# Two attention stages of a two-layer diffusion step: when a low part, a PSUM bank and a set of weights are put in the queues

## The chip, the cores and the metric

The kernel is one program on one core of a Trainium2 chip. The metric is the device time of one execution in microseconds (us), as the median of several runs. The core has five instruction streams that matter here: PE (TensorE, matrix products and transposes; PEld is its weight loads), DVE (VectorE), ACT (ScalarE), POOL (GpSimd) and SP (SyncE, which here only issues DMAs). Each takes its instructions strictly in the order of the program; they wait for each other by semaphores.

## The reference, cut to what matters

One step of a trunk of two layers over 512 latent tokens and 128 context tokens of width 1024. Layer 0 mixes tokens by 2-D neighbourhood attention (NA), layer 1 by grouped-query attention (GQA, 16 query heads over 4 key heads); a gated ConvFFN follows each.

```python
for l in range(DEPTH):                                   # DEPTH = 2
    hp = rmsnorm(xp, norm_mix_pre[l]) * (1.0 + sc_ap) + sh_ap      # context
    hs = rmsnorm(xs, norm_mix_pre[l]) * (1.0 + sc_as) + sh_as      # latents
    if l % 2 == 0:
        qp, kp, vp = na_qkv(hp, na_w_qkv[i]); op = blocked_attention(qp, kp, vp)
        qs, ks_, vs = na_qkv(hs, na_w_qkv[i])
        os_ = neighbourhood_attention(qs, ks_, vs, cache_k, cache_v, na_rpb[i])
        w_o = na_w_o[i]
    else:
        qp, kp, vp = gqa_qkv(hp, ...); op = blocked_attention(qp, kp, vp)
        qs, ks_, vs = gqa_qkv(hs, ...); qs, ks_ = axial_rope(qs), axial_rope(ks_)
        os_ = blocked_attention(qs, concat(ks_, cache_k), concat(vs, cache_v))
        w_o = gqa_w_o[i]
    xp = xp + g_ap * rmsnorm(op @ w_o, norm_mix_post[l])
    xs = xs + g_as * rmsnorm(os_ @ w_o, norm_mix_post[l])
    ...                                                  # gated ConvFFN, again with a residual
```

## The kernel before, in words

All products that carry weights or latent rows run in three passes over split numbers: a value x is held as a high part `hi` (a rounded copy, made by ACT) and a low part `lo = x - hi` (a subtraction, on DVE or POOL), and `passes` adds hi·hi, hi·lo and lo·hi. So every weight (`wsplit`: load `wr`, high part `wh`, low part `wl`) and every attention output costs one ACT copy and one subtraction before PE can use it.

PE's order is the order in which the program is written: `pe()` chains each matmul and transpose to the one before. The other engines' instructions are put in order by a scheduler from their readiness and their place in the program. Two calls bend that order, without adding a wait for data: `behind(a, b)` puts instruction a later than b on their engine, and `tc.keep_in_program_order(a)` puts it later than whatever the program wrote last for that engine. An engine runs its queue strictly in order, so what stands first and isn't ready holds back all behind it.

PSUM has eight banks of 128 x 512 f32. `Banks` hands them out first in, first out: `get` takes the bank that was returned longest ago, and `put` returns one at the place of the program where it is called. The next owner of a bank waits until the last reader of the old owner is done.

**GQA, layer 1.** After the projections four banks serve the scores (two tiles `d0` and `d1` of two banks each) and four go round among all else. The attention is cut into 32 units u: head `2*(u//4) + u%2`, half `u//2 % 2` of the latent rows. A unit has two score tiles (`scores(0)`, `scores(1)`: products `s`, DVE reduction `nmg` L1796, ACT exponential `gp` L1799, DVE reciprocal `rcg` L1801, POOL scaling `gp` L1802) and three transposes (`turns(0..2)`: 4, 4 and 2 PE turns into a bank `tp`, then a copy `pk` out of it: turn 0 by ACT L1813, turn 1 by DVE L1815, turn 2 by ACT or DVE). `GORDER` writes the order by hand:

```python
GORDER = ("s0 p v s1 t0".split(), "s0 l1 l2 t0 s1 t1 t2".split())   # even u, odd u
```

where s0, s1 are the scores of unit u + 2, t0, t1, t2 the turns of unit u, l1, l2 the last two turns of unit u - 1, p a leftover step of the query transposes or of the context attention, and v is `values`: the products of units u - 2 and u - 1 (two heads, one half) with the values, into a bank `po`. `po` is taken with the first half (`hf == 0`) and closed with the second (`hf == 1`): ACT writes the high part `ph` (L1832), DVE the low part `pl` (L1833), and the bank goes back. The list `held` carries instructions that a later `scores(i)` puts behind its reduction. The context columns of the same output come from `opr` and are split on POOL (L1840, L1841).

**NA, layer 0.** The heads' attention steps are interleaved with the projections by `ORDER`: each `f` runs one part of the queue `work` (`stream()`), whose last item is the key projection of head pair 7, in eight parts (first half of the rows in parts 0 to 3, second half in 4 to 7; `k_put` then splits the keys, `kp` is the context's key copy). At parts of this last item named in `OW` the first half of the output weights (`m0.weights(0, u)`) is split, pinned in program order. `o_split(p)` (L1097) splits the attention output of pair p into `oh` and `ol`: pairs 0 and 1 after head 11, the next after head 12, when the memory of the projections' input is free.

**First ConvFFN's end.** For the last tile of rows (t = 4) `after(i)` splits the four GQA key and value weights between the last products, while DVE and POOL finish tile 3 (`residual`, `ro` the reciprocal root, `shifted` L421).

Of the kernel before, what the change touches and what calls it, by code (L numbers as in the profile page):

```python
# [14 lines left out]
ALU = mybir.AluOpType  # L15
# [7 lines left out]
NS = 512  # L23
# [16 lines left out]
NPT = 6  # L40
NPK = 6
NAR = 2
OW = {0: 0, 2: 1, 7: 2}
OEARLY = 2
TH = 322
PLAIN = 2
# [58 lines left out]
def hybrid_step(ctx: ExitStack, tc: tile.TileContext, A, O):  # L105
# [57 lines left out]
    def x_in(t):  # L163
        return A["x_sample"][0, t * P : (t + 1) * P, :] if t < 4 else A["x_prompt"][0]

    queue, lowered = [], []


    def wsplit(src, a, b, low=None, own=None, pin=False, after=None, high=None, low_after=None):
        q = own or wp  # L170
        raw = wp.tile([P, a, b], F32, tag="wr", name="wr")
        i = nc.sync.dma_start(raw, src)
        if queue:
            behind(i, queue.pop())
        hi = q.tile([P, a, b], F32R, tag="wh", name="wh")
        i = nc.scalar.copy(hi, raw)  # L176
        lo = q.tile([P, a, b], F32R, tag="wl", name="wl")
        j = (low or nc.vector).tensor_sub(lo, raw, f32(hi))  # L178
        if high:
            behind(i, high[0])  # L180
        if after:
            behind(i, after[0])
            behind(j, after[1])
        lowered[:] = [j]
        if low_after and not low:
            behind(j, low_after)
        if pin:
            tc.keep_in_program_order(i)
            tc.keep_in_program_order(j)
        return hi, lo  # L190
# [150 lines left out]
    class Finish:  # L341
# [75 lines left out]

        def shifted(self, t):
            xm, r = self.xm[t]
            self.moved = [  # L420
                nc.vector.scalar_tensor_tensor(  # L421
                    xm[:, c], xm[:, c], r, self.sh[:, c], op0=ALU.mult, op1=ALU.add
                )
                for c in HALF
            ]
            return self.moved[0]

        def last(self, copied, added, low):

# [51 lines left out]
    vpool = l_na.enter_context(pool("nav", 3))  # L481
    tpool = l_na.enter_context(pool("nat"))
    mask = tpool.tile([P, 2, 32, 8], F32, name="mask")
    kput, plast, qput, splits = [], [], [], []
    wqkv = A["na_w_qkv"][0]

    def na_v_tile():
# [362 lines left out]
    with l_na:  # L850
# [50 lines left out]
        def na_qk_items(p):  # L901
# [20 lines left out]
            def k_put(c0, c1, src):  # L922
                for b in range(2):
                    own, oth = own_oth(b)
                    i = nc.scalar.copy(d["kh"][b][own, c0:c1], src[own])
                    j = (nc.scalar.copy if p else nc.vector.tensor_copy)(d["kh"][b][oth, c0:c1], src[own])
                    n = nc.vector.tensor_sub(d["kl"][b][own, c0:c1], src[own], f32(d["kh"][b][own, c0:c1]))
                while splits and c0 == 0:
                    for x, y in zip(splits.pop(), (j, n)):
                        behind(x, y)  # L930
                if not p:
                    kput[:] = [i]

            def part(which, half, k0):
# [12 lines left out]
                if which == 0:  # L947
                    if half == 0:
                        d["qs"] = [ap.tile([P, QW], F32R, tag=f"qs{b}", name=f"qs{b}") for b in range(2)]
                    pieces = [(slice(64 + cs.start, 64 + cs.stop), slice(0, nq))]  # L950
                    if half == 1:
                        pieces.append((slice(0, 64), slice(NS - 64 - cs.start, NS - cs.start)))
                    for qc, pc in pieces:
                        for b in range(2):
                            own, oth = own_oth(b)
                            q = d["qs"][b]
                            j = nc.scalar.activation(q[own, qc], pp[own, pc], AF.Copy, scale=-0.125)
                            i = nc.vector.scalar_tensor_tensor(
                                q[oth, qc], pp[own, pc], -0.125, f32(q[own, qc]),
                                op0=ALU.mult, op1=ALU.subtract,  # L960
                            )
                    qput[:] = j, i
                else:
                    if half == 0:
                        d["kh"] = [ap.tile([P, T + P], F32R, tag=f"kh{b}", name=f"kh{b}") for b in range(2)]
                        d["kl"] = kls[p % 2]
                        tk = bk.get("tk")
                        turn(tk[:, 0:P], d["kc"], ident)
                        k_put(CTX * P, CTX * P + P, tk[:, 0:P])
                        bk.put(tk)  # L970
                    if half == 1:
                        d["kp"] = ap.tile([P, P], F32, tag="kc", name="kp", bufs=2)
                        nc.scalar.copy(d["kp"], pp[:, NS - cs.start : T - cs.start])
                    k0 = cs.start + P * (cs.start >= CTX * P)
                    k_put(k0, k0 + nq, pp[:, 0:nq])
                    if half == 1:
                        qk_of[p] = (d["qs"], d["kh"], d["kl"])
# [116 lines left out]

        def o_split(p):
            hi, lo = osp0[p]
            i = nc.scalar.copy(hi, of0[p]), nc.vector.tensor_sub(lo, of0[p], f32(hi))  # L1097
            if p == 0:
                for j in range(2):
                    behind(i[j], qput[j])  # L1100
            elif p < OEARLY:
                splits.append(i)


        items, marks = [], {}
# [13 lines left out]
        def stream():  # L1119
            items[0][0]()  # L1120
            tail = None
            for n, (load, parts) in enumerate(items):
                for i, part in enumerate(parts):
                    part()
                    if n + 1 == len(items) and i in OW:
                        m0.weights(0, OW[i], None if i == 7 else nc.gpsimd)
                    if i == 1 and n + 1 < len(items):
                        items[n + 1][0]()
                    if i == 4 and tail:
                        tail()  # L1130
                        tail = None
                    yield
# [107 lines left out]
    def ffn(l, hT, hT_close, xold, xnew, nxt, todo, late, late_close, side, back, first, fin0, after=None):  # L1240
# [290 lines left out]
        for grp, (c0, c1) in (((0, 1, 2), HB[0]), ((3, 4), HB[1])):  # L1531
# [24 lines left out]
            for t in grp:  # L1556
# [7 lines left out]
                for i in range(tail):  # L1564
# [4 lines left out]
                        lds.append(load_dn(len(lds), *HB[1]))  # L1569
                    if t == 4 and after:  # L1570
                        after(i)
                        if not i:
                            behind(fin.moved[0], lowered[0])
                late.append(fin.end(t, acc[t][0], acc[t][1], fin.stat(acc[t][0])))
        fin.close()
        s.close()
# [186 lines left out]

        return [one, two, three]

    sps, sps_p, ta, un, held = ExitStack(), [], {}, {}, ([], [])

    class Unit:

# [34 lines left out]
        def turns(self, j):  # L1804
# [7 lines left out]
            if j == 0 or j == 2 and self.b == 0:  # L1812
                nc.scalar.copy(x, tp[:, 0:n])  # L1813
            else:
                nc.vector.tensor_copy(x, tp[:, 0:n])  # L1815
            bk.put(tp)
            for a, c in enumerate(cs):
                self.t[c] = x[:, 256 * a : 256 * a + 256]
# [1 line left out]
    def values(two):  # L1820
# [8 lines left out]
        if u.hf == 1:  # L1829
            p = u.p  # L1830
            hi, lo = osp1[p]
            nc.scalar.copy(hi[:, 0:NS], ta["po"])  # L1832
            held[0].append(nc.vector.tensor_sub(lo[:, 0:NS], ta["po"], f32(hi[:, 0:NS])))  # L1833
            bk.put(ta["po"])
            c, src = slice(NS, T), opr[:, p, :]
            if p == KC - 1:
                nc.scalar.copy(hi[:, c], src)
                nc.vector.tensor_sub(lo[:, c], src, f32(hi[:, c]))
            else:
                i = nc.gpsimd.tensor_scalar(hi[:, c], src, 1.0, None, op0=ALU.mult)  # L1840
                nc.gpsimd.tensor_sub(lo[:, c], src, f32(hi[:, c]))  # L1841
                tc.add_manual_dep(i.ins, last_rms[0].ins.name, no_sync, reason="order")

    ck = ap.tile([P, 256], F32, tag="ck", name="ck", bufs=1)
    nc.scalar.dma_start(ck, A["cache_gqa_k"][0, 0].rearrange("t h d -> t (h d)"))
# [74 lines left out]
    with ExitStack() as s:  # L1920
# [27 lines left out]
        for u in range(NU + 2):  # L1948
            if u + 2 < NU:
                un[u + 2] = Unit(u + 2)  # L1950
            for step in GORDER[u % 2]:
# [9 lines left out]
                elif step == "v" and u >= 2:  # L1961
                    values((un[u - 2], un[u - 1]))
            un.pop(u - 3, None)
            if u == WU:
                for k in range(4):
                    m1.weights(0, k, None)
# [105 lines left out]
```

## Time and profile before

| | |
|---|---|
| median of 3 runs | 1544.62 us (1543.17 to 1544.98) |
| the profiled execution | 1544.49 us, of which the recorded span is 1542.7 us |
| busy: PE, PEld | 1510.3 us (98%), 1342.4 us (87%) |
| busy: DVE, ACT, POOL | 1013.9 us (66%), 854.0 us (55%), 701.1 us (45%) |
| DMA | 243.99 MB, mean 158 GB/s |
| granted TensorE clock | 0.999 of full speed |

Where the stages lie in the span, in us: first layer's projections and attention to about 320, its output product and norms to 400, first ConvFFN to 811, GQA projections to 910, GQA attention 914 to 1037, its output product and norms to 1100, second ConvFFN to the end.

How to read the rows that follow: a row of a timeline is the start in us, the duration in us (of all merged instructions), the engine, the line of the kernel, the operation, output <- input, shapes and a count; in brackets the idle time of the engine just before it and what released it. A row of a list of waits is who waited, on whom, and then the total in us, the number of waits and the longest. A row of a table of windows is the stretch, its length, the busy time of PE, PEld, DVE, ACT and POOL with counts, the granted clock, the DMA engines' mean busy share and GB/s. When an instruction waits for several things, the releaser is the event that came last by the profile, which need not be the true one.

### The profile page before, as it was taken

The page shows a single profiled execution, that of the slowest core. Times are in us where ns is not written, and L with a number is a line of the kernel's source. Part 1 is how long each engine was busy: PE and PEld are TensorE (multiplying, and loading weights), DVE is VectorE, ACT ScalarE, POOL GpSimd, SP SyncE. Part 2 cuts the span into 40 slices and gives each one's busy share as a digit, 9 for nine tenths or more (in the row PEclk, how much of TensorE's full clock was granted, in tenths as well). Part 3 has the DMA queues.
Part 4 walks back from the last instruction along what each step waited for, and adds up shares of the span by engine and source line. Part 5 has one row for each costly group of instructions (what it writes and reads, how often), then busy time and mean ns, then how long its engine had stood idle before and what let it go on. Part 6 is the DMA issues. An engine that isn't in the chain of part 4 may idle for free.

```text
span 1542.7 us, 26131 instructions
## 1 busy us (share of the span) xinstructions
PE 1510.3 (98%) x9710; PEld 1342.4 (87%) x9710; DVE 1013.9 (66%) x1653; ACT 854.0 (55%) x1628; POOL 701.1 (45%) x602
## 2 busy tenths in 40 slices
PE   7999999999999999999999999999999999999998
PEld 5999989779999999988887877778999999998886
DVE  5544343659776676764747777672988887885454
ACT  5665564655655555644544447762666665564343
POOL 1655554332355445533544454432335666553433
PEclk9999999999999999999999999999999999999999
DMA  9755444263675664487574420005533334459664
GB/s 350 190 153 127 125 136 105 61 212 103 195 226 188 206 204 141 138 290 263 187 223 137 123 83 28 1 20 195 169 114 108 117 110 156 128 162 302 196 219 134
DMA packets 196667, 243.99 MB, mean 158 GB/s; under 512 B 11484, under 2 KB 153020, under 8 KB 196540
## 3 DMA queue, kind: packets, MB, share of 16 engines
q1 hardware_dynamic: 186924, 235.85, 47.6%
q10 hardware_dynamic: 9616, 6.48, 2.5%
q8 instruction: 76, 1.25, 0.3%
q14 instruction: 51, 0.42, 0.1%
HBM read 214.38 MB, written 26.34 MB: 156 GB/s over the span
## 4 chain that ended last, share of the span: by engine, by line
PE 64%; DVE 7%; issue 2%; POOL 2%; ACT 1%; DMA 1%; ACTq 0%; DVEq 0%; POOLq 0%
PE acc L117 19%; PE ux L117 17%; PE uz L117 9%; PE uy L117 5%; PE gp L117 3%; PE y L117 2%; PE s L117 2%; PE po L117 2%; PE tp L120 2%; PE ada L117 1%; DVE B L250 1%; DVE nmg L1796 1%; DMA gn<-in_gqa_k_norm 1%; DMA wr<-in_ffn_w_up 1%; DVE wl L178 0%
## 5 line engine op out<-in xcount | busy, mean ns | idle before, releaser
L178 POOL TENSOR_TENSOR wl<-wr,wh 128x1024 fp32r<-128x1024 f32 x70 | 171.2, 2450 | 238.5 <-ACT wh L176 238.3
L117 PE MATMUL ux<-B,wh 128*128 128x322 f32 x832 | 200.5, 312 | 0.7 <-ACT u L1349 0.4
L1294 POOL TENSOR_TENSOR wl<-wr,wh 128x1024 fp32r<-128x1024 f32 x76 | 181.5, 2410 | 42.1 <-ACT wh L1293 38.3
L1373 DVE SCALAR_TENSOR_TENSOR t<-C,cw,t 128x644 f32<-128x644 f32 x176 | 156.3, 888 | 51.2 <-ACT t L1370 50.7
L117 PE MATMUL acc<-wh,alo 128*128 128x512 f32 x440 | 172.0, 391 | 0.0
L117 PE MATMUL acc<-wh,ahi 128*128 128x512 f32 x440 | 171.9, 391 | 0.0
L117 PE MATMUL acc<-wl,ahi 128*128 128x512 f32 x440 | 171.8, 390 | 0.0
L176 ACT CAST wh<-wr 128x1024 fp32r<-128x1024 f32 x138 | 143.5, 1047 | 37.8 <-DMA wr<-in_ffn_w_down 26.0
L117 PE MATMUL uz<-B,wh 128*128 128x322 f32 x640 | 155.9, 312 | 0.0
L117 PEld LDWEIGHTS ux<-B,wh 128*128 128x128 f32 x832 | 143.5, 189 | 4.2 <-ACT u L1349 1.4
L1262 DVE TENSOR_TENSOR alo<-ain,ahi 128x384 fp32r<-128x384 f32 (+1 forms) x88 | 70.5, 819 | 94.0 <-ACT ahi L1260 93.7
L117 PE MATMUL ux<-B,wl 128*128 128x322 f32 x416 | 129.3, 311 | 0.2 <-DVE wl L799 0.2
L117 PE MATMUL qk<-hT,wh 128*128 128x384 f32 (+1 forms) x512 | 122.4, 315 | 0.0
L117 PEld LDWEIGHTS uz<-B,wh 128*128 128x128 f32 x640 | 110.9, 189 | 2.9 <-issue 0.8
L1293 ACT CAST wh<-wr 128x1024 fp32r<-128x1024 f32 x84 | 85.0, 1049 | 47.1 <-DVE wr L1318 46.7
L1294 POOL TENSOR_TENSOR vl<-wr,vh 128x1024 fp32r<-128x1024 f32 x38 | 98.5, 2593 | 20.0 <-ACT vh L1293 19.7
L178 DVE TENSOR_TENSOR wl<-wr,wh 128x1024 fp32r<-128x1024 f32 x68 | 91.3, 1352 | 19.3 <-ACT wh L176 18.7
L1370 ACT ACTIVATE t<-C,cw 128x644 f32<-128x644 f32 x88 | 78.6, 893 | 44.0 <-DVE C L1401 31.6
L1260 ACT CAST ahi<-ain 128x384 fp32r<-128x384 f32 (+1 forms) x88 | 39.7, 460 | 108.9 <-PE acc L117 96.6
L117 PE MATMUL uz<-B,wl 128*128 128x322 f32 x320 | 99.5, 311 | 0.4 <-POOL wl L1294 0.3
L117 PEld LDWEIGHTS acc<-wh,alo 128*128 128x128 f32 x440 | 82.6, 188 | 17.8
L117 PEld LDWEIGHTS acc<-wh,ahi 128*128 128x128 f32 x440 | 82.6, 188 | 17.8
(264 smaller groups left out, 3893.6 us busy)
## 6 DMA issues: line engine op xcount, KB each, us to landing
wr<-in_ffn_w_up SPq DMA_DIRECT2D x88, 512.0 KB
wr<-in_ffn_w_down SPq DMA_DIRECT2D x88, 512.0 KB
wr<-in_ada_w SPq DMA_DIRECT2D x72, 512.0 KB
act<-act SPq DMA_DIRECT2D x44, 321.0 KB
wr<-in_na_w_qkv SPq DMA_DIRECT2D x24, 512.0 KB
mod<-modrow SPq DMA_DIRECT2D x20, 512.0 KB
ain<-act SPq DMA_DIRECT2D x44, 192.0 KB
wf<-in_ada_w SPq DMA_DIRECT2D x16, 512.0 KB
```

Source lines behind the costliest of these rows:

```text
L117: pe(nc.tensor.matmul(*a, **k))
L120: pe(nc.tensor.transpose(*a, **k))
L176: i = nc.scalar.copy(hi, raw)
L178: j = (low or nc.vector).tensor_sub(lo, raw, f32(hi))
L250: return nc.vector.tensor_sub(lo, src, f32(hi))
L1260: pin(nc.scalar.copy(hi[:, 0 : c1 - c0], ain[:, 0 : c1 - c0]))
L1262: i = nc.vector.tensor_sub(lo[:, 0 : c1 - c0], ain[:, 0 : c1 - c0], f32(hi[:, 0 : c1 - c0]))
L1293: nc.scalar.copy(hl[0], src)
L1294: return low.tensor_sub(hl[1], src, f32(hl[0]))
L1370: nc.scalar.activation(t, taps(0), AF.Identity, bias=cw[:, 3, n : n + 1], scale=cw[:, 1, n : n + 1])
L1373: nc.vector.scalar_tensor_tensor(t, taps(d), cw[:, w, n : n + 1], t, op0=ALU.mult, op1=ALU.add))
L1796: self.red[i] = nc.vector.tensor_reduce(nm, sv, axis=AX.XY, op=ALU.min)
```

## The change

In GQA the low part `pl` of a closed pair is put behind the DVE copy of the next turn 1 (`held[2]`, popped in `turns` with j == 1) in place of the next reduction of `scores(0)`, and the bank of `po` is returned at the end of the odd unit that follows (`ta["old"]`). The context columns' splits on POOL are kept in program order, where they had been put behind the last reciprocal root of the projections. In NA the splits of the outputs of pairs 0 and 1 are no longer put behind the last query evictions (`qput`) and the key evictions of pair 7 (`splits`), and the third block of output weights is split after part 4 of the last item and not after part 7. At the end of the first ConvFFN `shifted` of tile 3 is no longer put behind the low part of the first key weights (`lowered`).

```diff
--- before.py
+++ after.py
@@ -40,7 +40,7 @@
 NPT = 6
 NPK = 6
 NAR = 2
-OW = {0: 0, 2: 1, 7: 2}
+OW = {0: 0, 2: 1, 4: 2}
 OEARLY = 2
 TH = 322
 PLAIN = 2
@@ -163,7 +163,7 @@
     def x_in(t):
         return A["x_sample"][0, t * P : (t + 1) * P, :] if t < 4 else A["x_prompt"][0]

-    queue, lowered = [], []
+    queue = []


     def wsplit(src, a, b, low=None, own=None, pin=False, after=None, high=None, low_after=None):
@@ -181,7 +181,6 @@
         if after:
             behind(i, after[0])
             behind(j, after[1])
-        lowered[:] = [j]
         if low_after and not low:
             behind(j, low_after)
         if pin:
@@ -417,13 +416,12 @@

         def shifted(self, t):
             xm, r = self.xm[t]
-            self.moved = [
+            return [
                 nc.vector.scalar_tensor_tensor(
                     xm[:, c], xm[:, c], r, self.sh[:, c], op0=ALU.mult, op1=ALU.add
                 )
                 for c in HALF
-            ]
-            return self.moved[0]
+            ][0]

         def last(self, copied, added, low):

@@ -481,7 +479,7 @@
     vpool = l_na.enter_context(pool("nav", 3))
     tpool = l_na.enter_context(pool("nat"))
     mask = tpool.tile([P, 2, 32, 8], F32, name="mask")
-    kput, plast, qput, splits = [], [], [], []
+    kput, plast = [], []
     wqkv = A["na_w_qkv"][0]

     def na_v_tile():
@@ -923,11 +921,8 @@
                 for b in range(2):
                     own, oth = own_oth(b)
                     i = nc.scalar.copy(d["kh"][b][own, c0:c1], src[own])
-                    j = (nc.scalar.copy if p else nc.vector.tensor_copy)(d["kh"][b][oth, c0:c1], src[own])
-                    n = nc.vector.tensor_sub(d["kl"][b][own, c0:c1], src[own], f32(d["kh"][b][own, c0:c1]))
-                while splits and c0 == 0:
-                    for x, y in zip(splits.pop(), (j, n)):
-                        behind(x, y)
+                    (nc.scalar.copy if p else nc.vector.tensor_copy)(d["kh"][b][oth, c0:c1], src[own])
+                    nc.vector.tensor_sub(d["kl"][b][own, c0:c1], src[own], f32(d["kh"][b][own, c0:c1]))
                 if not p:
                     kput[:] = [i]

@@ -954,12 +949,11 @@
                         for b in range(2):
                             own, oth = own_oth(b)
                             q = d["qs"][b]
-                            j = nc.scalar.activation(q[own, qc], pp[own, pc], AF.Copy, scale=-0.125)
-                            i = nc.vector.scalar_tensor_tensor(
+                            nc.scalar.activation(q[own, qc], pp[own, pc], AF.Copy, scale=-0.125)
+                            nc.vector.scalar_tensor_tensor(
                                 q[oth, qc], pp[own, pc], -0.125, f32(q[own, qc]),
                                 op0=ALU.mult, op1=ALU.subtract,
                             )
-                    qput[:] = j, i
                 else:
                     if half == 0:
                         d["kh"] = [ap.tile([P, T + P], F32R, tag=f"kh{b}", name=f"kh{b}") for b in range(2)]
@@ -1094,12 +1088,8 @@

         def o_split(p):
             hi, lo = osp0[p]
-            i = nc.scalar.copy(hi, of0[p]), nc.vector.tensor_sub(lo, of0[p], f32(hi))
-            if p == 0:
-                for j in range(2):
-                    behind(i[j], qput[j])
-            elif p < OEARLY:
-                splits.append(i)
+            nc.scalar.copy(hi, of0[p])
+            nc.vector.tensor_sub(lo, of0[p], f32(hi))


         items, marks = [], {}
@@ -1123,7 +1113,7 @@
                 for i, part in enumerate(parts):
                     part()
                     if n + 1 == len(items) and i in OW:
-                        m0.weights(0, OW[i], None if i == 7 else nc.gpsimd)
+                        m0.weights(0, OW[i], None if i == 4 else nc.gpsimd)
                     if i == 1 and n + 1 < len(items):
                         items[n + 1][0]()
                     if i == 4 and tail:
@@ -1569,8 +1559,6 @@
                         lds.append(load_dn(len(lds), *HB[1]))
                     if t == 4 and after:
                         after(i)
-                        if not i:
-                            behind(fin.moved[0], lowered[0])
                 late.append(fin.end(t, acc[t][0], acc[t][1], fin.stat(acc[t][0])))
         fin.close()
         s.close()
@@ -1763,7 +1751,7 @@

         return [one, two, three]

-    sps, sps_p, ta, un, held = ExitStack(), [], {}, {}, ([], [])
+    sps, sps_p, ta, un, held = ExitStack(), [], {}, {}, ([], [], [])

     class Unit:

@@ -1812,7 +1800,9 @@
             if j == 0 or j == 2 and self.b == 0:
                 nc.scalar.copy(x, tp[:, 0:n])
             else:
-                nc.vector.tensor_copy(x, tp[:, 0:n])
+                i = nc.vector.tensor_copy(x, tp[:, 0:n])
+                while j == 1 and held[2]:
+                    behind(held[2].pop(), i)
             bk.put(tp)
             for a, c in enumerate(cs):
                 self.t[c] = x[:, 256 * a : 256 * a + 256]
@@ -1830,16 +1820,15 @@
             p = u.p
             hi, lo = osp1[p]
             nc.scalar.copy(hi[:, 0:NS], ta["po"])
-            held[0].append(nc.vector.tensor_sub(lo[:, 0:NS], ta["po"], f32(hi[:, 0:NS])))
-            bk.put(ta["po"])
+            held[2].append(nc.vector.tensor_sub(lo[:, 0:NS], ta["po"], f32(hi[:, 0:NS])))
+            ta["old"] = ta.pop("po")
             c, src = slice(NS, T), opr[:, p, :]
             if p == KC - 1:
                 nc.scalar.copy(hi[:, c], src)
                 nc.vector.tensor_sub(lo[:, c], src, f32(hi[:, c]))
             else:
-                i = nc.gpsimd.tensor_scalar(hi[:, c], src, 1.0, None, op0=ALU.mult)
-                nc.gpsimd.tensor_sub(lo[:, c], src, f32(hi[:, c]))
-                tc.add_manual_dep(i.ins, last_rms[0].ins.name, no_sync, reason="order")
+                tc.keep_in_program_order(nc.gpsimd.tensor_scalar(hi[:, c], src, 1.0, None, op0=ALU.mult))
+                tc.keep_in_program_order(nc.gpsimd.tensor_sub(lo[:, c], src, f32(hi[:, c])))

     ck = ap.tile([P, 256], F32, tag="ck", name="ck", bufs=1)
     nc.scalar.dma_start(ck, A["cache_gqa_k"][0, 0].rearrange("t h d -> t (h d)"))
@@ -1961,6 +1950,8 @@
                 elif step == "v" and u >= 2:
                     values((un[u - 2], un[u - 1]))
             un.pop(u - 3, None)
+            if u % 2 and "old" in ta:
+                bk.put(ta.pop("old"))
             if u == WU:
                 for k in range(4):
                     m1.weights(0, k, None)
```

## The prediction

> **What bounds the kernel now.** I read the page's first part, then the list of TensorE's waits cut to the attention of the second layer (905 to 1035 us), then the timelines of the engines around single waits.
>
> ```profile
> PE 1510.3 (98%) x9710; PEld 1342.4 (87%) x9710; DVE 1013.9 (66%) x1653; ACT 854.0 (55%) x1628; POOL 701.1 (45%) x602
> 930.00:1000.00 70.00, 66.07 (x521) 54.08 (x518) 50.71 (x109) 49.79 (x122) 32.10 (x43) 1.00 0.05 16
> PE tp L120 <- DVE rcg L1801: 6.8, 7, 1.1
> PE tp L120 <- POOL gp L1802: 1.4, 2, 0.9
> PE s L117 <- ACT gp L1799: 0.7, 1, 0.7
> ```
>
> PE is busy 98% of the span, so only its gaps can be won. In 930 to 1000 us it is idle 3.9 of 70 us at a granted clock of 1.00, while DVE (50.7) and ACT (49.8) have room, and DMA is at 5%: work there runs by the chain between engines, not by loads. The three rows of waits list all of PE's larger gaps in this attention: 6.8 us in seven waits of one kind, 1.4 us in two of another, 0.7 us in one.
>
> One of the seven, in order of time, PE first, then DVE, ACT and POOL:
>
> ```profile
> 932.52 0.60 PE L120 MATMUL tp<-ident,gp 128*128 128x128 f32 x4
> 932.88 0.54 PE L117 MATMUL s<-gkh,gq 128*128 128x320 f32 x2
> 933.55 0.82 PE L120 MATMUL tp<-ident,gp 128*128 128x128 f32 x6
> 935.32 0.63 PE L120 MATMUL tp<-ident,gp 128*128 128x128 f32 x4 [0.95 <-DVE rcg L1801]
> 936.37 0.82 PE L120 MATMUL tp<-ident,gp 128*128 128x128 f32 x6
> 942.16 1.25 PE L120 MATMUL tp<-ident,gp 128*128 128x128 f32 x10
> 933.75 0.82 DVE L1796 TENSOR_REDUCE nmg<-s 128x1 f32<-128x640 f32 x1 [0.20 <-PE s L117]
> 934.49 0.68 DVE L1833 TENSOR_TENSOR pl<-po,ph 128x512 fp32r<-128x512 f32 x1
> 935.09 0.15 DVE L1801 RECIPROCAL rcg<-sug 128x1 f32<-128x1 f32 x1
> 935.16 0.67 DVE L1815 COPY pk<-tp 128x512 f32<-128x512 f32 x1
> 936.57 0.82 DVE L1796 TENSOR_REDUCE nmg<-s 128x1 f32<-128x640 f32 x1 [0.67 <-PE s L117]
> 933.16 0.59 ACT L1813 COPY pk<-tp 128x512 f32<-128x512 f32 x1 [0.61 <-PE tp L120]
> 935.34 1.57 POOL L1802 TENSOR_SCALAR gp<-gp,rcg 128x640 f32<-128x640 f32 x2 [2.36 <-DVE rcg L1801]
> ```
>
> Read it against the code. The x4 at 932.52 is step t0 of an even unit, the x6 at 933.55 are l1 (four turns) and l2 (two), the x4 at 935.32 is t0 of the odd unit, the x6 at 936.37 are t1 and t2. The view names rcg, but a turn reads gp, which POOL makes from rcg, and the next gp starts at 935.34, after the turn: rcg can't be its input. The bank can. Four banks go round first in, first out. Where values() closes a pair (hf = 1) it gives po's bank back at once, as the fourth in the queue: t0, l1 and l2 take the other three, and t0 of the odd unit gets po's own bank, which DVE reads until pl ends at 935.17. PE starts 0.15 us later. rcg ends at 935.24 and only happens to be the last DVE event ahead. In the odd unit of the other half of a pair (942.16, ten turns without a gap) po is held, three banks go round, and t0 gets the bank of the even t0, long copied.
>
> **The change, part by part, against this execution (1544.49 us, of which 1542.7 are the span; the median of the runs is 1544.62, 0.13 more).**
>
> *Bank one unit later, and pl behind the copy of l1.* The odd t0 then gets the bank of the even t0, which ACT has copied at 933.75; PE reaches it at 935.32 - 0.95 = 934.37. The wait goes: 7 waits, 6.8 us. What is late next: t1 takes the bank of l1. PE is there 936.37 - 935.32 = 1.05 us after t0, at 935.42. With pl out of its way, DVE copies l1 from 934.49 to 935.16, and with the 0.15 us seen above the bank is free at 935.31: 0.11 us to spare, 0.05 short if rcg goes first. I take 0.05 for each, 0.3 us in all. pl now runs behind that copy, in the 0.67 us for which DVE sat idle before 936.57; the reduction behind it starts some 0.3 us late, and who waits for it (exp, rcg, gp) is needed in the next odd unit, some 6 us later (942.16): nothing. The next po now takes another bank than its old one: in the units with an extra step p (a quarter of them at most, about five) that of t1, whose copy moves to about 936.6 to 937.25, with PE there at about 937.2: 0 to 0.25 each, I take 0.1, 0.5 in all. The last of the seven lies just ahead of the first output products, which wait for their weights already:
>
> ```profile
> 1037.62 0.50 PE L117 MATMUL y<-wl,ph 128*128 128x512 f32 x1 [0.18 <-DVE wl L178]
> ```
>
> PE would come 0.95 us earlier to a chain of splits that moves by less; I take 0.4 us off. Sum of this part: -6.8 + 0.3 + 0.5 + 0.4 = -5.6, between -6.8 and -4.0 (0.2 at every t1, 0.25 at five po, 0.9 at the end).
>
> *The context part of the output (opr) on POOL.* Today only the last rms is ahead of these splits, so those of four pairs run as soon as that is done:
>
> ```profile
> 914.44 1.04 POOL L1840 TENSOR_SCALAR ph<-opr 128x128 fp32r<-128x128 f32 x2
> 915.44 0.87 POOL L1841 TENSOR_TENSOR pl<-opr,ph 128x128 fp32r<-128x128 f32 x2
> 916.28 1.23 POOL L1840 TENSOR_SCALAR ph<-opr 128x128 fp32r<-128x128 f32 x2
> 917.48 0.86 POOL L1841 TENSOR_TENSOR pl<-opr,ph 128x128 fp32r<-128x128 f32 x2
> 918.33 3.13 POOL L1802 TENSOR_SCALAR gp<-gp,rcg 128x640 f32<-128x640 f32 x4
> 919.18 0.33 PE L120 MATMUL tp<-ident,gp 128*128 128x128 f32 x1 [0.91 <-POOL gp L1802]
> 919.96 0.55 PE L120 MATMUL tp<-ident,gp 128*128 128x128 f32 x3 [0.45 <-POOL gp L1802]
> ```
>
> Four gp stand in a queue behind 3.9 us of splits, and PE waits 0.91 + 0.45 us for the first two. In program order each pair's split stands in its own even unit, behind the gp of s0. POOL starts at 914.4 with gp, done at 916.0, before PE asks at 918.3: -1.4 us, between -1.4 and 0 (if something else is as late). In the units 1.0 us of splits fits the 2.36 us for which POOL sat idle before 935.34: nothing; without that cover seven times 1.0.
>
> *NA: splits of pairs 0 and 1 free, third weights three parts earlier.* ACT, DVE and PE at the end of the first layer's projections:
>
> ```profile
> 267.42 1.92 ACTq L862 DMA_DIRECT2D tr<-in_k_rpb  x3
> 269.38 0.49 ACT L957 ACTIVATE qs<-qk 64x384 fp32r<-64x384 f32 x1 [2.16 <-POOL p L1053]
> 273.19 0.73 ACT L1097 CAST oh<-of 128x640 fp32r<-128x640 f32 x1
> 277.98 0.72 ACT L1097 CAST oh<-of 128x640 fp32r<-128x640 f32 x1
> 278.73 0.27 ACT L973 COPY kp<-qk 128x128 f32<-128x128 f32 x1
> 282.39 1.04 ACT L176 CAST wh<-wr 128x1024 fp32r<-128x1024 f32 x1
> 283.33 1.35 ACT L1097 CAST oh<-of 128x640 fp32r<-128x640 f32 x2
> 279.05 0.33 PE L120 MATMUL tk<-ident,kp 128*128 128x128 f32 x1 [0.78 <-ACT kp L973]
> 285.93 0.50 PE L117 MATMUL y<-wh,ol 128*128 128x512 f32 x1 [1.09 <-DVE ol L1097]
> ```
>
> The weights' hi (1.04 on ACT at 282.39) and lo (on DVE behind it) stand ahead of the splits of pairs 2 and 3. Moved up, they stand behind the first half's key copies, about 278.0, and those splits come about 1 us earlier: the wait of 1.09 goes. But they now stand ahead of kp, for which PE waits 0.78 already: + 1.04, less the 0.72 of the hi at 277.98, which leaves its place: + 0.3. The raw weights are loaded long before, and no load on SP lies between the two places. The two free hi copies (0.73 + 0.72) can start once the rows of the last modulation, over whose memory they lie, are stored, near the evictions of the last queries (269.38): hidden if they fit beside the loads that ACT issues from 267.42, else these evictions and the bank they hold come up to 1.45 later. I take 0.3. Sum: -1.09 + 0.3 + 0.3 = -0.5, between -1.9 (kp gains too) and + 1.4.
>
> *First FFN's end: shifted no longer behind the first key weights.*
>
> ```profile
> 810.37 1.22 DVE L178 TENSOR_TENSOR wl<-wr,wh 128x1024 fp32r<-128x1024 f32 x1
> 812.31 1.41 DVE L421 SCALAR_TENSOR_TENSOR xm<-xm,ro,mod 128x512 f32<-128x512 f32 x2 [0.72 <-POOL ro L381]
> 813.64 3.49 DVE L178 TENSOR_TENSOR wl<-wr,wh 128x1024 fp32r<-128x1024 f32 x3
> 817.18 0.73 PE L117 MATMUL gp<-wl,hT 128*128 128x512 f32 x2 [0.40 <-DVE wl L178]
> ```
>
> shifted waits for ro until 812.3, after this split is done, so the same order stands to reason: 0. If shifted is put first, all four splits end 1.2 us later, and PE's 0.40 becomes 1.6: 0 to + 1.2.
>
> Sum: -5.6 - 1.4 - 0.5 + 0 = -7.5, and 1544.49 - 7.5 = 1537.0 us. No load of the attention limits it (DMA 5%), and the weights and rows behind it are asked for by work that moves along, so the gain lasts to the end.
>
> **Rivals.** *The name in the view is right:* the odd t0 waits for something in DVE's chain that stays, and moving pl and the bank wins nothing. For it: seven rows name rcg. Against: gp starts after the turn, and the ten turns at 942.16 need no wait. Only POOL's and NA's parts are left: 1544.5 - 1.9 = 1542.6.
>
> *Three banks are too few (slower):* po's bank is now out in nearly every unit, and in each of the 15 odd units behind the first t1 must wait for the copy of l1. It decides from (6.8 + 1.4 + 0.5) / 15 = 0.58 us a unit on; at the 0.95 that t0 pays today it costs 15 x 0.95 = 14.2 against these 8.7: 1550. Against: the ten turns at 942.16 run on three banks today with no gap. The Trainium skill's page "PSUM — Partial Sum Buffer" (Summary: rules for kernel authors) says to evacuate PSUM promptly because it is tight; this change does the opposite, and by that rule the 1550 would be the outcome. The ungapped row speaks against it here.
>
> *NA's older order costs:* the free hi copies go in front of the last query evictions and the weights in front of kp, 1.45 + 1.04 with no gain at 285.93: + 2.5 in place of - 0.5, 1540.0. For it: ACT runs without a gap there.
>
> **Chances.** Forecast 0.72 (its own range 1534 to 1540), the name is right 0.10, three banks 0.04, NA costs 0.14. The predicted time is that of the forecast. The range 1534 to 1541.8 leaves out the first two rivals and a little of the forecast's lower tail, 0.2. 0.2% is 3.1 us, about what a measurement tells from no change: faster (below 1541.5) 0.82, same 0.12, slower 0.06.
>
> **What would show it.** Of the seven waits of tp about none is left in 930 to 1035, and pl follows a pk copy; a remainder would stand at the x6 behind the odd t0. No split of opr at 914 to 918, and no wait of tp for gp at 919. In NA no wait for ol near 285.9, and kp behind a weights' hi. The prediction is wrong if t0 keeps its gap with pl moved, if gaps move to t1 or po in every unit, or if the new places on ACT open gaps in NA of more than 2 us.

## The result: 1535.55 us, and the profile after

| | before | after |
|---|---|---|
| median of 6 runs each, on one chip | 1544.36 us (1543.17 to 1545.60) | 1535.55 us (1534.39 to 1536.63) |
| the profiled execution: time, span | 1544.49, 1542.7 us | 1535.05, 1533.3 us |

The ratio is 0.9943, with a 95% interval of 0.9930 to 0.9956: 8.8 us less. The forecast was 7.5 less, 1537.0.

The first part of the page, then the stretch of 70 us of the attention that answers to 930 to 1000 of before, then the whole list of PE's waits from 900 to 1031 us, all of the changed kernel:

```profile
PE 1511.8 (99%) x9710; PEld 1344.4 (88%) x9710; DVE 1016.9 (66%) x1653; ACT 853.2 (56%) x1628; POOL 703.1 (46%) x602
927.00:997.00 70.00, 69.51 (x540) 56.74 (x538) 53.86 (x115) 52.11 (x129) 34.85 (x47) 1.00 0.05 16
PE s L117 <- ACT gp L1787: 0.7, 1, 0.7
PE y L117 <- DVE wl L178: 0.2, 1, 0.2
```

PE's idle time in the 70 us fell from 3.9 to 0.5 us at the same clock. Of the three rows of before, the seven waits named rcg and the two for gp are gone; the single wait of s (0.7) stands as it was. (In the rows of the changed kernel the line numbers are lower, by 10 to 12 in the attention: L1787 is L1799 of before, L1803 is L1815, L1823 is L1833; and by 1 to 6 in the stages ahead of it.)

The same pair of units as in the prediction, from the timelines of the changed kernel; PE, then its weight loads, DVE and POOL:

```profile
929.20 1.25 PE L120 MATMUL tp<-ident,gp 128*128 128x128 f32 x10
931.04 0.87 PE L120 MATMUL tp<-ident,gp 128*128 128x128 f32 x6
...
931.03 0.64 PEld L120 LDWEIGHTS tp<-ident,gp 128*128 128x128 f32 x6 [0.22 <-DVE pk L1803]
933.02 1.92 PEld L117 LDWEIGHTS po<-pk,gvt 128*64 128x64 f32 x20 [0.32 <-DVE pk L1803]
...
930.29 0.69 DVE L1803 COPY pk<-tp 128x512 f32<-128x512 f32 x1
930.90 0.68 DVE L1823 TENSOR_TENSOR pl<-po,ph 128x512 fp32r<-128x512 f32 x1
931.49 0.15 DVE L1789 RECIPROCAL rcg<-sug 128x1 f32<-128x1 f32 x1
931.56 0.81 DVE L1784 TENSOR_REDUCE nmg<-s 128x1 f32<-128x640 f32 x1
932.29 1.01 DVE L1803 COPY pk<-tp 128x512 f32<-128x512 f32 x2
...
928.61 0.54 POOL L1830 TENSOR_SCALAR ph<-opr 128x128 fp32r<-128x128 f32 x1
929.23 0.46 POOL L1831 TENSOR_TENSOR pl<-opr,ph 128x128 fp32r<-128x128 f32 x1
```

The six turns l1, l2 and the four of t0, two groups with 0.95 us between them before, are one row of ten without a gap. pl follows the copy of l1, and rcg follows pl: rcg now ends at 931.64, 1.2 us *after* the tenth turn, so it never was what t0 waited for. What is late next are the weight loads of t1 (x6) and of po, which wait 0.2 and 0.3 us for copies.

**A ledger.** PE runs the same 9710 instructions in the same order in both kernels, so the starts of each can be subtracted, and every gap that goes or comes is a step in the difference:

| place (time before) | step, us |
|---|---|
| start-up, to 33 us | +1.1 |
| NA, 273.8 to 291.8 | -1.9 |
| 355 | -0.2 |
| two turns of the GQA projections, 836.8 and 843.7 | -1.5 |
| first units of the attention, 919.2 and 920.0 | -1.8 |
| the rest of the attention: seven gaps -7.9, given back between them +2.7 | -5.2 |
| all other | 0.0 |
| end | -9.5 |

The start-up differs from one execution to the next: at 262 us the traces of e1 to e6 below, which leave it alone, are 0.3 to 1.6 us later than that of before. A part of it is the clock: from 20.0 to 23.5 us the granted clock was 1.00 in before's trace and 0.51 in that of the changed kernel.

PE's waits from 262 to 300 us (NA), before and then after:

```profile
PE y L117 <- DVE ol L1097: 1.1, 1, 1.1
PE tk L120 <- ACT kp L973: 0.8, 1, 0.8
PE tp L120 <- POOL pp L771: 0.7, 1, 0.7
PE sp L117 <- DVE kl L927: 0.2, 1, 0.2
```
```profile
PE tp L120 <- DVE qs L953: 1.0, 1, 1.0
PE tp L120 <- POOL p L1047: 0.5, 1, 0.5
PE tk L120 <- ACT kp L967: 0.2, 1, 0.2
```

Four waits, 2.8 us, became three of 1.7. The new one, for qs, is that of the queries behind the two free copies, as the timeline of ACT after shows:

```profile
269.83 0.73 ACT L1091 CAST oh<-of 128x640 fp32r<-128x640 f32 x1 [1.58 <-POOL p L1047]
270.47 0.48 ACT L952 ACTIVATE qs<-qk 64x384 fp32r<-64x384 f32 x1
270.86 0.71 ACT L1091 CAST oh<-of 128x640 fp32r<-128x640 f32 x1
272.04 0.49 ACT L952 ACTIVATE qs<-qk 64x384 fp32r<-64x384 f32 x1 [0.47 <-DVE qs L953]
...
279.24 1.05 ACT L176 CAST wh<-wr 128x1024 fp32r<-128x1024 f32 x1
280.31 0.27 ACT L967 COPY kp<-qk 128x128 f32<-128x128 f32 x1
```

### The profile page after: what moved, and what is told of

It is laid out like the page before. It is cut to its first block, busy times and chain, and to the rows that moved or that the text cites. A ratio compares the mean times of both kernels' runs of the same rounds, so it can differ in the third digit from the quotient of the medians.

```text
span 1533.3 us, 26124 instructions
## 1 busy us (share of the span) xinstructions
PE 1511.8 (99%) x9710; PEld 1344.4 (88%) x9710; DVE 1016.9 (66%) x1653; ACT 853.2 (56%) x1628; POOL 703.1 (46%) x602
## 4 chain that ended last, share of the span: by engine, by line
PE 85%; DVE 8%; ACT 2%; issue 2%; POOL 1%; DMA 1%; DVEq 0%; SPq 0%; ACTq 0%; POOLq 0%
PE acc L117 19%; PE ux L117 17%; PE uz L117 9%; PE qk L117 6%; PE y L117 6%; PE gp L117 5%; PE uy L117 5%; PE vp L117 4%; PE po L117 4%; PE s L117 3%; PE tp L120 3%; PE ada L117 2%; PE tr L120 1%; DVE nmg L1784 1%; DVE B L249 1%
## 5 line engine op out<-in xcount | busy, mean ns | idle before, releaser
L1252 DVE TENSOR_TENSOR alo<-ain,ahi 128x384 fp32r<-128x384 f32 (+1 forms) x88 | 74.3, 860 | 91.3 <-ACT ahi L1250 90.4
L117 PEld LDWEIGHTS acc<-wl,ahi 128*128 128x128 f32 x440 | 82.6, 188 | 17.9
```

Of the source, the lines that this page charges most:

```text
L117: pe(nc.tensor.matmul(*a, **k))
L1252: i = nc.vector.tensor_sub(lo[:, 0 : c1 - c0], ain[:, 0 : c1 - c0], f32(hi[:, 0 : c1 - c0]))
```

## The experiments

Times are medians beside runs of the kernel before on the same chip, with the ratio and its 95% interval. "Aligned" is the ledger's method.

| kernel | us | before | ratio (95%) | us less or more |
|---|---|---|---|---|
| e1, GQA bank and pl | 1538.69 | 1544.28 | 0.9965 (0.9952 to 0.9977) | -5.6 |
| e2, opr on POOL | 1543.12 | 1544.28 | 0.9993 (0.9984 to 1.0002) | -1.2 |
| e3, NA | 1542.58 | 1544.28 | 0.9989 (0.9980 to 0.9997) | -1.7 |
| e4, shifted free | 1543.83 | 1544.28 | 0.9999 (0.9990 to 1.0008) | -0.5 |
| e5, bank alone | 1541.14 | 1543.74 | 0.9984 (0.9975 to 0.9993) | -2.6 |
| e6, pl alone | 1549.39 | 1543.74 | 1.0035 (1.0021 to 1.0048) | +5.7 |
| e7, after, bank back sooner | 1535.04 | 1543.74 | 0.9943 (0.9931 to 0.9956) | -8.7 |
| e8, after, NA splits as before | 1536.46 | 1543.74 | 0.9950 (0.9937 to 0.9962) | -7.3 |
| e9, after, pl behind t2 | 1534.24 | 1544.91 | 0.9939 (0.9927 to 0.9952) | -10.7 |
| e10, after, NA splits behind qs | 1539.48 | 1544.91 | 0.9966 (0.9953 to 0.9978) | -5.4 |
| e11, e9 and e10 together | 1539.30 | 1544.91 | 0.9968 (0.9956 to 0.9980) | -5.6 |

**The four parts, each alone on the kernel before (e1 to e4).**

e1, the bank one unit later and pl behind the copy of l1:

```diff
-            held[0].append(nc.vector.tensor_sub(lo[:, 0:NS], ta["po"], ...))
-            bk.put(ta["po"])
+            held[2].append(nc.vector.tensor_sub(lo[:, 0:NS], ta["po"], ...))
+            ta["old"] = ta.pop("po")
...
+            if u % 2 and "old" in ta:
+                bk.put(ta.pop("old"))
```

> Only the GQA part of the change: pl behind the copy of l1 and po's bank returned one unit later; NA, opr and the first FFN as before. Theory A (the odd t0 waits for po's own bank, which pl still reads): the seven waits of tp named rcg go, small waits at the products po (0.3 to 0.5 us in about four units) and at the first output products come up; between the starts of the first pairs' turns and the output products PE gains about 5.3 us, as the two traces show (PE's instructions of before and after lie 4.3 us apart after the POOL stretch and 9.6 us apart at the end of the attention), so the median falls by 5 to 6 us. Theory B (the name rcg is right, the wait is another link of DVE's chain): the seven waits stay, 0 us. Theory C (the four pieces help only together): less than 3 us.

The seven waits are gone from its list of waits, all others of the attention stand as before, and the stage gave 5.2 us aligned: theory A. Nearly two thirds of the gain of the whole change.

e2, the splits of opr on POOL in program order:

```diff
-                tc.add_manual_dep(i.ins, last_rms[0].ins.name, no_sync, reason="order")
+                tc.keep_in_program_order(...)     # both instructions
```

> Only the opr splits on POOL in program order, all else as before. Theory A (four gp stand behind the splits in POOL's queue): no split at 914 to 918 us, no wait of tp for gp near 919 (0.91 and 0.45 us before), a gain of 1.4 to 1.8 us. Rival (other work of that stretch is as late): the waits change their name and the time stays within 0.5 us. In the units POOL's splits cost nothing by A; by the rival of POOL's queue the next gp is late by up to 1.0 us in seven units.

Its interval reaches 1, so the time alone settles nothing. The trace does: the two waits for gp at 919 are gone, and the step there is 1.8 us aligned, as in the whole change. From 930 to 1037 us nothing of it is lost, so the splits in their new places in the units cost nothing that PE shows.

e3, the weights three parts earlier and the splits of pairs 0 and 1 free:

```diff
-OW = {0: 0, 2: 1, 7: 2}
+OW = {0: 0, 2: 1, 4: 2}
...
-            if p == 0:
-                for j in range(2):
-                    behind(i[j], qput[j])
-            elif p < OEARLY:
-                splits.append(i)
```

> Only the NA part: output splits of pairs 0 and 1 free, third weights after part 4. Theory A, from the aligned traces of before and after: a new wait of about 1 us of tp for qs near 275 (two hi copies stand in front of the last query evictions), against the waits for kp, kl and ol (0.78, 0.23, 1.09 us) and for pp (0.74 us) that go or shrink; net 1.9 us faster. Theory B (these waits come back a little later, at the next norms): nothing is left by 330 us, time within 0.5 us.

The list of its waits in NA is that of the changed kernel, row for row (1.0 for qs, 0.5 for p, 0.2 for kp), and the stage gave 1.9 us aligned, which last to the end.

e4, shifted no longer behind the low part of the first key weights:

```diff
-                        if not i:
-                            behind(fin.moved[0], lowered[0])
```

> Only the order of shifted and the first key weights' low part at the end of the first FFN. In the trace of after shifted goes first, ro comes 1.1 us earlier on POOL, and the four low parts end where they did (816.0 against 817.05 less the 1.1 by which all lies earlier). Theory A: no effect on PE there, 0 us, and the 1.4 us that PE gains in after at two turns tk (836.8 and 843.7 before) come from when the loads of gn landed in that execution, so they are here by chance or not at all. Theory B: those 1.4 us belong to this edit, because ACT and POOL are done earlier and the loads of gn go out earlier: about 1.4 us faster, and no wait of tk.

PE's wait there is 0.4 us in both, and the times can't be told apart. But shifted went first, which the prediction had not expected (how this cost nothing is told below, with that step). In e4's trace a gap of the GQA projections is shorter by 0.7 us, and in e1 and e2, which don't touch that stage either, the two of them by 1.2 and 1.5 in all: the ledger's -1.5 at 837 and 844 is the luck of the profiled execution of before and belongs to no part of the change.

The four parts alone sum to -9.0, and the whole gave -8.8: within their intervals they add up. Aligned, the stages gave 5.2, 1.8, 1.9 and 0, which is 8.9.

**The two halves of the GQA edit (e5, e6).** e5 has the lines of `bk.put` alone, e6 those of `held[2]` alone.

> Of the GQA part only the bank: po's bank is returned one unit later, pl stays behind the reduction and so ahead of the copy of l1; the rest as before. Theory A (the wait is for the bank): the odd t0 gets the bank of the even t0 and no longer waits; t1 then waits for the copy of l1, which ends at 935.83 against PE's 935.42, with 0.15 us from copy to PE some 0.56 us, seven times: 6.8 - 3.9 = 2.9 us gained, less up to 1.5 us at po in the units with a step p: 1.4 to 2.9 us faster, seven waits of tp left, later in the unit. Theory B (the order of DVE's queue is all): 0 us, the wait stays at t0.

> Of the GQA part only the order: pl behind the copy of l1, po's bank returned at once as before; the rest as before. Theory A: the odd t0 still gets po's own bank and must wait for pl, which now starts after the copy of l1 (935.16) and ends at 935.84: seven waits of 0.95 become about 1.6, 4 to 5 us slower. Theory B (DVE's order is all, the bank is nothing): the gain of the whole part, 5.6 us.

PE's waits of t0 and t1 from 910 to 1040 us, in e5 and then in e6:

```profile
PE tp L120 <- DVE pk L1815: 3.3, 7, 0.6
```
```profile
PE tp L120 <- DVE rcg L1801: 12.0, 7, 1.7
```

One of e6's seven, DVE and then PE:

```profile
935.82 0.68 DVE L1835 TENSOR_TENSOR pl<-po,ph 128x512 fp32r<-128x512 f32 x1
936.41 0.15 DVE L1801 RECIPROCAL rcg<-sug 128x1 f32<-128x1 f32 x1
936.64 0.63 PE L120 MATMUL tp<-ident,gp 128*128 128x128 f32 x4 [1.71 <-DVE rcg L1801]
```

With the bank alone t0 runs through, and the wait comes at t1, for the copy of l1 that stands behind pl: 3.3 us in seven, in place of 6.8. With the order of DVE alone, t0's seven waits grow from 6.8 to 12.0, since pl, the last reader of the bank that t0 gets, now ends later. rcg is named there again, and again the bank is what is waited for: from the end of pl to the start of t0 it is 0.15 us in all seven waits of before and in all seven of e6, while from the end of rcg it is 0.08 us in thirteen of them and 0.02 in the other. Neither half is the change: -2.6 and +5.7 alone, -5.6 together. Theory A both times; aligned, the attention gave 3.3 us in e5 and lost 5.2 in e6, each a little more than was expected.

**What is left of the gaps (e7, e9).** e7 is the changed kernel with the bank returned right behind t0 of the odd unit (that of the last pair, behind which no such t0 comes, at the very end), e9 with pl behind the copy of turn 2 in place of turn 1:

```diff
+                    if u % 2 and step == "t0" and "old" in ta:        # e7
+                        bk.put(ta.pop("old"))
...
-                while j == 1 and held[2]:
+                while j == 2 and held[2]:                             # e9
```

> The kernel after, with po's bank returned right behind the odd t0 in place of the end of that unit, so that the next po or the step before it gets a bank that has been free for long and not the one that t1 was just copied from. Theory A (what PE loses again at the next products, 0.35 to 0.5 us in four units of the trace of after, is the wait for the copy of t1): these four losses go, 1.2 to 1.8 us faster than after, 1533.8 to 1534.4. Rival (PE loses them to the weight loads of these products whatever the bank): as after, 1535.5.

> The changed kernel with pl put behind the DVE copy of turn 2 of the next odd unit, in place of the copy of l1 (turn 1); the bank still goes back at the end of that unit. Theory A (what is left of the gaps, 0.3 us a pair ahead of po and sp, comes from pl's 0.68 us standing ahead of s1's reduction and of the copies of t1 and t2): those reductions and copies come 0.6 us earlier, the weight loads of po and sp no longer wait for pk (now 0.6 us in 2 and 0.5 us in 2), and each of seven pairs gives back 0.2 to 0.35 us: 1.4 to 2.5 us below the changed kernel, some 1533.3. Rival B (the gaps come from the copies themselves and from exp behind the reduction, not from pl): within 0.5 us of the changed kernel, with the same rows of waits. Rival C (pl ends too late for the owner of po's old bank): a new wait of tp for pl in the even unit, 0.3 to 0.7 in each of seven, 2 to 5 us slower.

Both missed. In e7 the four waits of po and sp for pk are gone, 0.15 to 0.3 us each and 0.9 in all, but at three places a little later the scores start 0.16 us later, where they wait for the exponential before them:

```profile
938.83 0.56 PE L117 MATMUL s<-gkh,gq 128*128 128x320 f32 x2 [0.22 <-ACT gp L1787]
```

Aligned with the changed kernel, the attention is 0.5 us shorter, less than half of what theory A said. The end is the same (0.0) only because a gap of the GQA projections, at 844, which the edit doesn't touch, is 0.7 us longer in that execution. In e9 pl's row moved as meant, and the weight loads of po and sp no longer wait for pk. But those of tp do more, 3.2 us in 14 in place of 2.5 in 12, those of s and po put down to issue grew from 4.7 us in 18 to 6.2 in 23, and the first output product waits 0.6 for its weights in place of 0.2: aligned, the attention gave nothing (the trace is 1.4 us ahead from the start-up on, and 1.0 at the end). Its median is 1.3 lower than that of the changed kernel, within the intervals of both. So what is left there is no longer one wait. Both runs show gaps that close at po and sp and open, in part or in full, at the scores, the turns or the output products; that the chains of DVE and ACT as a whole now run at PE's pace is the reading that fits both, and isn't shown beyond this.

**Where NA's splits stand (e8, e10, e11).** e8 is the changed kernel with the splits of pairs 0 and 1 held back as before; in e10 both are behind the last query evictions.

> The kernel after, with the output splits of pairs 0 and 1 in NA put behind the last query evictions and key evictions as before; the third weights stay after part 4. Theory A (the free splits cost the wait of tp for qs near 275 and pay it back by leaving the place ahead of kp): no wait of 0.96 near 275, but kp behind two more ACT copies, a wait of tk of 1.2 to 1.8 us, and the gain at ol (1.09 us) stays: 0 to 1 us slower than after, 1535.5 to 1536.5. Rival (the early weights alone bring NA's gain, the free splits only cost): 1 us faster than after, 1534.5.

> The changed kernel with the splits of NA's output pairs 0 and 1 both put behind the last query evictions (none behind the keys, and the third weights stay at their earlier place). Theory A (the two free high copies, 0.73 and 0.71 us on ACT, and low parts, 0.83 each on DVE, stand in front of the last query evictions and are all of the new wait of 0.96 for qs): that wait goes, and the splits fit before the weights' copies: 1.0 us earlier at 276 us, of which 0.5 to 1.0 stay to the end of NA. Rival B (moved behind, they push the key copies and kp, as the splits behind the keys did): the 1.0 is given back at the wait for kp or kl by 285 us, 0 to 0.5 slower in all.

PE's waits from 262 to 300 us, in e8 and then in e10:

```profile
PE tk L120 <- ACT kp L973: 1.7, 1, 1.7
```
```profile
PE tp L120 <- POOL p L1048: 1.9, 1, 1.9
PE tk L120 <- ACT kp L968: 1.8, 1, 1.8
```

In both the wait for qs is gone and turns up in full, and more, at kp. In e10 the rest of ACT's chain is late as well, and p behind it costs 1.9, where it was 0.5. Behind that wait PE runs at half its clock for about 3 us; first that stretch of e10, then the changed kernel from the same products on:

```profile
290.00:293.00 3.00, 3.00 (x11) 2.42 (x10) 1.18 (x6) 1.65 (x5) 1.04 (x1) 0.50 0.42 161
```
```profile
287.50:290.50 3.00, 3.00 (x19) 2.52 (x18) 3.00 (x9) 2.31 (x11) 0.98 (x1) 1.00 0.43 122
```

At a granted clock of 0.50 the matmuls start about twice as far apart, and PE falls back by another 1.6 us. In all e10 is 4 us slower than the changed kernel, where rival B said 0 to 0.5. Theory A of e10 fell, and its rival was too mild. e8 comes out 0.9 slower than the changed kernel, which the intervals don't separate; aligned it is 0.1 slower by 300 us and 0.3 at the end. That is theory A of e8, near the lower end of its 0 to 1 us; its rival fell. Free or held as before, the splits come to nearly the same: free, they cost 1.1 at qs and 0.6 at p, and give back 1.6 at kp and 0.2 at kl. Only the place behind the last query evictions is shown to be worse. What NA gained came from the early weights: e8, which has them with the splits held, is 1.8 us ahead of before there, aligned.

> The changed kernel with both of the edits just described (pl behind turn 2, both free splits behind the last query evictions). If theory A holds for both, 2 to 3.5 us below the changed kernel, some 1532.5, faster than both kernels; with rival B for both, within 0.7 us of it.

e11 is e10's time, as follows from the two. No kernel tried is shown to beat the changed one.

## Why the prediction came out

**GQA: -5.6 forecast, -5.6 in e1.** The mechanism is shown by e1, e5 and e6: the bank, not the name in the view. The terms inside were off and cancelled, so that the size fits as well as it does is luck. The seven waits were taken at their 6.8 us; PE gained 7.9 (the steps of the ledger there are 1.1 to 1.2 us each, beside the view's 0.95: the view counts a gap only from the end of the turn before it, and in an ungapped row the next turn starts before that end). What was put against it, 0.3 at t1, 0.5 at po and 0.4 at the end, 1.2 in sum, was 2.7: t1 gives back 0.2 in six pairs and not 0.05, and po or sp 0.15 to 0.35 in five and not 0.1. The 0.4 at the end did not come: the output product y waits 0.19 us for its weights after and 0.18 before. The bound of -4.0 given with this sum doesn't follow from its own terms: 0.2 at seven t1, 0.25 at five po and 0.9 at the end leave -3.25.

**opr on POOL: -1.4 forecast, -1.8 aligned, -1.2 in the time of e2.** gp is no longer behind the splits, and nothing took the place of the wait. The ten turns are one row, the two gp that the last four of them read are done by 913.5, and POOL has gp alone:

```profile
914.91 1.25 PE L120 MATMUL tp<-ident,gp 128*128 128x128 f32 x10
...
911.90 1.58 POOL L1790 TENSOR_SCALAR gp<-gp,rcg 128x640 f32<-128x640 f32 x2
915.02 0.80 POOL L1790 TENSOR_SCALAR gp<-gp,rcg 128x640 f32<-128x640 f32 x1 [1.54 <-DVE rcg L1789]
```

**NA: -0.5 forecast, -1.9 aligned, -1.7 in e3.** The signs of the steps were right but for one, and the sum was mis-sized. The wait for ol went, with 1.5 us for the 1.09 taken. The free copies did come in front of the query evictions, 1.1 where 0.3 was taken (the bound was 1.45). The key copy kp ended at 279.00 before and 280.58 after, 0.5 us later once the 1.1 of the start-up is taken off, near the 0.3 forecast; but PE was 1.1 later by then, behind qs, so the wait shrank by 0.6 where the sum had +0.3 added. That is the step that failed: two delays in a row were added, though the second is hidden by the first. And two waits behind them, for kl and pp, had not been counted: -0.4 and -1.0, against +0.5 new for p. By e8 the two edits of this part were not of one kind: the early weights bring the gain, and the free splits change it by 0.1 us. (No run has the free splits with the weights late.) The total of -7.5 fell short of -8.8 by about what this part was short of.

**First FFN's end: 0 forecast, 0 measured, by a wrong reason.** "The same order stands to reason" was wrong, and so was the +1.2 for the other order. shifted went first, but ro, for which it waits, came 1.1 us earlier, so the four low parts end within 0.1 us of where they did. DVE and POOL after:

```profile
810.14 1.42 DVE L420 SCALAR_TENSOR_TENSOR xm<-xm,ro,mod 128x512 f32<-128x512 f32 x2 [0.81 <-POOL ro L380]
811.47 4.63 DVE L178 TENSOR_TENSOR wl<-wr,wh 128x1024 fp32r<-128x1024 f32 x4
...
809.11 0.35 POOL L373 TENSOR_SCALAR v<-sso,v 128x1 f32<-128x1 f32 x1 [0.33 <-ACT junk L371]
809.55 0.55 POOL L380 TENSOR_TENSOR ro<-v,mhalf 128x1 f32<-128x1 f32 x1
```

**The rivals.** "The name in the view is right" fell with e1 and e6. "Three banks are too few" did not come: the copies keep up, at 0.2 us a t1 and not 0.95. The rule of the Trainium skill's page "PSUM — Partial Sum Buffer" (Summary: rules for kernel authors), to evacuate promptly, stood in the prediction for that outcome; the 1535.55 goes against it here, since in this first in, first out ring the order of the returns decided (e1, e5, e6), and not how long one bank is out. "NA's older order costs" was right in its first half (1.1 at qs) and wrong in its sum.

## What to carry to other kernels

Where banks go round first in, first out, ask for each wait whose bank the waiter gets and who reads it last, before believing the releaser that the view names: an event that merely ended last ahead of it is named just as well. Move the return and the last reader together; either alone moved the wait (e5) or lengthened it (e6). Delays in a row on one engine's path don't add up: the longer one hides the other. Once the large waits are gone, a gap that is closed at one place comes back, in part or in full, at the next (e7, e8, e10). When a part of a change joins two edits, run each alone: of NA's two, one brought the gain and the other next to nothing (e8).

## What the runs showed of the hardware

A small POOL instruction took four times as long beside a DVE subtraction that reads two operands from SBUF. Before:

```profile
810.24 1.40 POOL L374 TENSOR_SCALAR v<-sso,v 128x1 f32<-128x1 f32 x1 [0.34 <-ACT junk L372]
811.72 0.55 POOL L381 TENSOR_TENSOR ro<-v,mhalf 128x1 f32<-128x1 f32 x1
```

It ends at 811.64, 0.05 us after the subtraction wl (810.37, 1.22 us, shown in the prediction). Where that subtraction comes later, as in the rows of after above and in e4, whose only edit is this order, the same instruction takes 0.35 us, and ends 0.13 us after DVE's operation ahead of it (808.04 to 809.33 in after). The Trainium skill's page "SBUF — State Buffer" (section "SBUF: two separate sides") says that DVE and GpSimd share a pair of ports as an exclusive lock, and that of a DVE operation with two SBUF inputs and a GpSimd one that reads SBUF the first to start keeps it while the other blocks; the 1.40 against 0.35 agrees with a lock. The rows don't show which of the two takes it first: POOL's record starts 0.13 us ahead of DVE's, and POOL is the one that waits.

The granted clock of PE fell to 0.50 for about 3 us behind a wait of 1.85 us in e10, with one of 1.75 us 8 us ahead of it (the row is shown with e10), and in e11, which has the same two waits (1.85 and 1.73). It stayed at 1.00 behind a single wait of 1.74 us in e8 and behind the seven of up to 1.72 in e6, 16 us or more apart. What decides it isn't shown by these runs.
